# Query and key projections of a hybrid decoder: high and low part of the input in one 512-column matmul

## The chip, the cores and the metric

The kernel runs on one core of a Trainium2 chip. The metric is device time in microseconds (us) of one execution; the time before is the median of 3 runs. One execution was also recorded by the hardware profiler, and everything said of the inside of the kernel is read from that record.

## The reference, cut to what matters

Two layers work on a sequence of 256 tokens with width 1024. Each layer normalises its input, multiplies it by one wide matrix, feeds the column groups of the product to three kinds of heads, and maps the heads' output back into the residual. All arrays are float32.

```python
D_MODEL = 1024; BATCH = 1; SEQ = 256; DEPTH = 2; HEAD_DIM = 64
A_HEADS = 8; B_HEADS = 4; C_HEADS = 4
SPLIT_SIZES = [A_WIDTH] * 4 + [B_WIDTH] * 4 + [C_WIDTH] * 5 + [C_HEADS, C_HEADS]
...
def hybrid_layer(x, norm_w, w_in, conv_w, conv_b, gate_bias, ret_norm_w, mlstm_norm_w, w_out):
    h = rmsnorm(x, norm_w)
    proj = jnp.matmul(h, w_in).astype(jnp.float32)
    (aq, ak, av, ag, bq, bk, bv, bg, cq, ck, cv, co, cg, ci, cf) = jnp.split(proj, cuts, axis=-1)
    ya = moba_attention(split_heads(aq, A_HEADS), split_heads(ak, A_HEADS), split_heads(av, A_HEADS))
    ya = merge_heads(ya) * jax.nn.silu(ag)
    yb = retention(rotate(split_heads(bq, B_HEADS), pos), rotate(split_heads(bk, B_HEADS), pos),
                   split_heads(bv, B_HEADS))
    yb = head_norm(yb, ret_norm_w) * jax.nn.silu(bg)
    qk = jax.nn.silu(causal_dwconv(jnp.concatenate([cq, ck], axis=-1), conv_w, conv_b))
    ...
    yc = mlstm(split_heads(cq_c, C_HEADS), split_heads(ck_c, C_HEADS), split_heads(cv, C_HEADS), i_pre, f_pre)
    yc = head_norm(yc * split_heads(jax.nn.sigmoid(co), C_HEADS), mlstm_norm_w) * jax.nn.silu(cg)
    y = jnp.concatenate([ya, yb, yc], axis=-1)[:, :s].astype(x.dtype)
    return x + jnp.matmul(y, w_out)
```

With 256 tokens the block-sparse attention (A) is causal softmax attention over one block with a distance bias, retention (B) is one chunk, and the mLSTM (C) is computed by the kernel over the whole sequence at once.

## The kernel before, in words

**Split matmuls.** The large products are made with a faster float32 format of the TensorE (`float32r`). To keep the precision, each operand is split into a high part, rounded to that format by an ACT copy, and a low part, the remainder, by a DVE subtraction: `hi` and `lo` for the weights, `xh` and `xl` for the input (`split_x`, L416), `yh` and `yl` for the heads' output. A product is then three matmuls into the same PSUM bank: high by high, high by low, low by high.

**Weights.** `CHUNKS` (L38) cuts the columns of the input matrix into 17 pieces a layer, and the output matrix into 4, in the order in which they are worked through. `loader` (L378) fetches each piece by DMA into one of three `raw` tiles; `splitter` (L434) makes `hi` (ACT) and `lo` (DVE) of it in two halves of 1024 columns, in three tiles each, so it can be at most three chunks ahead of the TensorE.

**Projection.** `project` (L560) walks over the chunks of a layer. The query and key chunks (aq0, ak0, bq, bk, cq, ck, aq1, ak1; 256 columns each) are made transposed, channels in partitions and the 256 tokens along the free axis: the weights are the stationary operand, the input is the moving one. For each of 8 k-tiles and each of the two halves of 128 channels there are three matmuls of 256 columns (L586 to L590), and both halves go into one PSUM bank of 512 columns. The first pair of layer 0 (i = 0, 1) is worked through together as its inputs arrive. The other chunks (cvif, bvco, av, cgbg, ag) are wide: the input is stationary, the weights move, 512 columns at a time (264 for cvif), and a chunk takes two banks. The output projection of layer 0 again moves 256 columns.

**PSUM.** There are eight banks: four with the tag `pj` for projections and four with the tag `mx` for everything else (scores, transposes, head outputs).

**Evacuation.** When a query or key chunk is done, `evac_aqk` (L714), `evac_bqk` (L973) or `evac_cqk` (L842) takes it out of its bank, once the row norm of the layer is known (event `rs`; for B also `cs`), since the norm's factor is multiplied in here. A: a DVE product into a `t512` tile. B: four ACT copies of 32 partitions, which swap the halves of each head for the rotation, and a DVE product into a second `t512` tile. C: a DVE product into the convolution's buffer `cpad`. Then `stack_w` and `stack_m` (L738, L750) split the result again into `st`, `zu` and `zd` tiles for the score matmuls of `dots` (L772). The copies in there are made with `CP` (L267), which lets ACT or DVE do it.

**Order.** The order on each engine is not written down line by line. Every piece of work is a generator, and a list scheduler (`Sched`, L111) with a cost for each instruction picks the one that could start first, with a priority as tie-breaker, while the program is built; the engines then run their instructions in this fixed order. It counts a matmul as max(107, columns / 2.4) + 3 ns (L274). Tiles and banks are handed out by `acq` in the order of asking and given back with `sc.release`. An evacuation starts with priority -1, ahead of the splits (0, or 6 where they are far ahead), and goes to 2 when it has freed its bank.

All instructions pass through helpers, so the profile puts TensorE matmuls on L280, transposes on L285, VectorE on L259, ScalarE on L265 and DMAs on L288. Tiles tell them apart.

Of the kernel before, what the change touches and what calls it, by code (L numbers as in the profile page):

```python
# [11 lines left out]
F32R = mybir.dt.float32r  # L12
AF = mybir.ActivationFunctionType
OP = mybir.AluOpType
AX = mybir.AxisListType

S = 256
D_ = 1024
EPS = 1e-6
KT = 8  # L20
# [208 lines left out]
def trunk(ctx: ExitStack, tc: tile.TileContext, xp: bass.AP, w: bass.AP, fn: bass.AP,  # L229
# [5 lines left out]
    sc = Sched()  # L235

    def sb_tile(shape, name, dt=F32):
        return cp.tile(shape, dt, name=name)
# [11 lines left out]
    def V(name, out, *a, after=None, fast=False, **k):  # L250
        n = _n(a[0]) if name == "tensor_reduce" else _n(out)
        cost = n / (1.92 if fast else 0.96) + 69
        if name in ("tensor_scalar", "scalar_tensor_tensor"):
            cost += 61 * (isap(a[1]) + (isap(a[2]) if name == "tensor_scalar" else 0))
        if name == "tensor_tensor_reduce":
            cost = n / 1.3
        if name == "reciprocal":
            cost = 6.4 * n + 69
        return op("dve", cost, lambda: getattr(nc.vector, name)(out, *a, **k), after)  # L259
# [30 lines left out]
    def wait(ev):  # L290
        return ("wait", ev)
# [4 lines left out]
    def acq(tag):  # L296
        return ("acq", tag)
# [4 lines left out]
    x = px[:, P_N:].rearrange("p (k t) -> p k t", t=S)  # L302
# [5 lines left out]
    vc = sb_tile([128, 2, 4, 65], "vc")  # L308
    vb = sb_tile([128, 2, 4, HD], "vb")
    cpad = sb_tile([128, 4, 3 + S], "cpad")  # L310
    xh = sb_tile([128, KT, S], "xh", F32R)
    xl = sb_tile([128, KT, S], "xl", F32R)
    yh = sb_tile([128, KT, S], "yh", F32R)
    yl = sb_tile([128, KT, S], "yl", F32R)
    sel = sb_tile([128, 4, 128], "sel", F32R)
# [7 lines left out]
    cr = sb_tile([128, S], "cr")  # L323
# [45 lines left out]
    def E(*key):  # L369
        if key not in evs:  # L370
            evs[key] = Event()
        return evs[key]

    raws, his, los = {}, {}, {}
    at_chunk = [0]
# [184 lines left out]
    def project():  # L560
        for l in range(DEPTH):
# [3 lines left out]
            while c < len(CHUNKS):  # L565
                name, cols, k0, k1 = CHUNKS[c]
                i = base + c
                n = len(cols)
                if name[1] in "qk":
                    m = 2 if i == 0 else 1  # L570
                    ii = range(i, i + m)
                    at_chunk[0] = i + m - 1
                    ps = []
                    for q in ii:
                        p = yield acq("pj")
                        ps.append(p)
                    if i:
                        for q in ii:
                            yield wait(E("w", q, 0))
                    hv = [his[q][:, :2048].rearrange("p (k c) -> p k c", k=KT) for q in ii]  # L580
                    lv = [los[q][:, :2048].rearrange("p (k c) -> p k c", k=KT) for q in ii]
                    for k in range(KT):
                        yield wait(E("x", l, k))
                        for z in range(m):
                            yield wait(E("wk", z, k) if i == 0 else E("w", i + z, k // 4))
                            for t in range(2):  # L586
                                cs = slice(t * 128, (t + 1) * 128)
                                for q, (a, b) in enumerate(((hv[z], xh), (hv[z], xl), (lv[z], xh))):
                                    e = yield M(ps[z][:, t * 256:(t + 1) * 256], a[:, k, cs], b[:, k, :],
                                                k + t + q == 0, k == KT - 1 and q == 2)  # L590
                    for z, q in enumerate(ii):
                        sc.release("hi", his.pop(q), e)
                        sc.release("lo", los.pop(q), e)
                        nm = names[c + z]
                        sc.spawn(EVAC[nm[:2]](l, nm, ps[z]), -1, e)
                    c += m
                else:
                    ps = []
                    for b in range(2):
                        p = yield acq("pj")  # L600
                        ps.append(p)
                    parts = 2 if name.endswith("_0") else 1
                    for j in range(parts):
                        i = base + c + j
                        at_chunk[0] = i
                        _, _, k0, k1 = CHUNKS[c + j]
                        yield wait(E("w", i, 0))
                        h, lo = his[i], los[i]
                        hv = h[:, :(k1 - k0) * n].rearrange("p (k c) -> p k c", c=n)
                        lv = lo[:, :(k1 - k0) * n].rearrange("p (k c) -> p k c", c=n)  # L610
                        for k in range(k0, k1):
                            yield wait(E("w", i, (k - k0) * 2 // (k1 - k0)))
                            for b in range(2):
                                bs = slice(b * 128, (b + 1) * 128)
                                for q, (a, r) in enumerate(((xh, hv), (xh, lv), (xl, hv))):
                                    e = yield M(ps[b][:, :n], a[:, k, bs], r[:, k - k0, :], k == 0 and q == 0,
                                                k == KT - 1 and q == 2)
                        sc.release("hi", h, e)
                        sc.release("lo", lo, e)
                        del his[i], los[i]  # L620
                    sc.spawn(EVAC[name[:2]](l, name, ps), -1, e)
                    c += parts
# [88 lines left out]
    def row(a):  # L711
        return rrow.unsqueeze(1).to_broadcast([128, 2, S])

    def evac_aqk(l, name, p):  # L714
        yield wait(E("rs", l))
        t = yield acq("t512")
        if name[1] == "q":
            yield wait(E("tab"))
            for u in range(2):
                j = T_QS + 2 * int(name[2]) + u  # L720
                e = yield V("scalar_tensor_tensor", b2(t)[:, u], b2(p)[:, u], tb[:, j:j + 1], rrow, op0=OP.mult,
                            op1=OP.mult)
        else:
            e = yield V("tensor_tensor", b2(t), b2(p), row(0), op=OP.mult)
        sc.release("pj", p, e)
        yield prio(2)
        yield from (stack_w if name[1] == "q" else stack_m)(l, name, t)
        if name[1] == "k":
            g = int(name[2])
            yield wait(E("qk", l, f"aq{g}"))  # L730
            box = [0]
            for u in range(2):
                sc.spawn(pair_a(l, g, u, box), 2)
# [105 lines left out]
        sc.release("mx", pt, e)  # L839
        sc.set(done, e)  # L840

    def evac_cqk(l, name, p):  # L842
        t = 0 if name == "cq" else 2
        yield wait(E("rs", l))
        if l:
            yield wait(E("conv", l - 1, name))
        e = yield V("tensor_tensor", cpad[:, t:t + 2, 3:], b2(p), row(0), op=OP.mult)
        sc.release("pj", p, e)
        yield prio(2)
        z = yield acq("t512")  # L850
        zv = b2(z)
        for u in range(2):
            o = P_CW + l * 16 + (t + u) * 4
            ob = P_CB + l * 4 + t + u
            yield A(zv[:, u], cpad[:, t + u, 3:], AF.Identity, scale=pr[:, o + 3:o + 4], bias=pr[:, ob:ob + 1])
            for j in (2, 1, 0):
                e = yield V("scalar_tensor_tensor", zv[:, u], cpad[:, t + u, j:j + S], pr[:, o + j:o + j + 1], zv[:, u],
                            op0=OP.mult, op1=OP.add)
        sc.set(E("conv", l, name), e)
        th = yield acq("t512")  # L860
        yield A(th, z, AF.Tanh, scale=0.5)
        e = yield V("scalar_tensor_tensor", th, th, 1.0, z, op0=OP.add, op1=OP.mult)
        sc.release("t512", z, e)
        yield from (stack_w if name == "ck" else stack_m)(l, name, th)
# [105 lines left out]
        sc.release("sb", wt, e)  # L970
        sc.set(done, e)

    def evac_bqk(l, name, p):  # L973
        yield wait(E("cs", l))
        yield wait(E("tab2"))
        sw = yield acq("t512")
        for c in range(4):
            d = c ^ 1
            e0 = yield A(sw[d * 32:(d + 1) * 32, :], p[c * 32:(c + 1) * 32, :], AF.Copy)
        r_ = yield acq("t512")  # L980
        e = yield V("tensor_tensor", b2(r_), b2(p), cr.unsqueeze(1).to_broadcast([128, 2, S]), op=OP.mult)
        sc.release("pj", p, e)
        yield prio(2)
        yield V("tensor_tensor", b2(sw), b2(sw), sr.unsqueeze(1).to_broadcast([128, 2, S]), op=OP.mult)
        e = yield V("tensor_tensor", r_, r_, sw, op=OP.add)
        sc.release("t512", sw, e)
        yield from (stack_w if name == "bk" else stack_m)(l, name, r_)
        if name == "bk":
            yield wait(E("qk", l, "bq"))
            sc.spawn(group_b(l), 2)  # L990
# [180 lines left out]
```

## Time and profile before

| what | value |
|---|---|
| median of 3 runs | 305.57 us (305.52 to 305.85) |
| the profiled execution | 305.33 us |
| its span, first to last instruction | 303.6 us |
| instructions | 5195 |
| query and key matmuls of 256 columns (`pj<-xh,hi`, `pj<-xh,lo`, `pj<-xl,hi`) | 3 x 256 |
| wide matmuls of 512 columns on the input | 3 x 128 |

In the views, PE is the TensorE's matmuls, PEld its weight loads, DVE the VectorE, ACT the ScalarE, POOL the GpSimd, SP the queue that issues the DMAs. A row of the timeline gives start and duration in us, engine, line, operation and output<-inputs with the shapes; a row of the groups gives the total in us and the mean in ns of one, and then the idle time of the engine ahead of it. `x3` is a count. A row of the waits has the waiting engine, tile and line, what it waited for, and total, times and longest in us.

The query and key chunks lie at 4 to 44 us and 75 to 98 us in layer 0, and at 152 to 191 and 224 to 243 in layer 1; the wide chunks lie between and behind them, the output projections at 127 to 151 and from 272.

### The profile page before, as it was taken

Reading aid. Unit: us, or ns where it says so; the run is one execution under the profiler, and the core shown is the slowest. Engines: PE = TensorE matmul, PEld = TensorE weight load, DVE = VectorE, ACT = ScalarE, POOL = GpSimd, SP = SyncE. Lnnn points to the kernel's source line nnn. Section 1 sums busy time; section 2 is a strip of 40 time slices with the busy share of each in tenths; the row PEclk is TensorE's granted clock in tenths of the full one; section 3 lists DMA queues with packets and bytes.
Section 4 is the critical chain, followed back from the end, with each engine's and each line's share of the span. In section 5 each row is a group of like instructions: output and inputs, shape, how many; then the busy total and the mean of one; then the engine's idle time right before and its main releaser. Section 6 shows DMA issues by size and latency. Waiting matters only on the chain.

```text
span 303.6 us, 5195 instructions
## 1 busy us (share of the span) xinstructions
PE 294.3 (97%) x2016; PEld 270.5 (89%) x2016; DVE 251.3 (83%) x523; ACT 187.6 (62%) x311; POOL 15.0 (5%) x19
## 2 busy tenths in 40 slices
PE   8899999999999999999999999999999999999992
PEld 6899999887999888899999999988899988888881
DVE  3969799998989998766889799998988998767553
ACT  5958975997244656535656879487445475664332
POOL 5000000000002020000020000000002002000010
PEclk9999999999999999999999999999999999999997
DMA  6999256545620444841617706547340536250003
GB/s 201 380 384 369 123 173 245 178 139 211 221 85 0 140 138 138 270 147 21 260 15 263 244 39 188 217 151 252 137 167 2 157 123 201 83 202 1 0 2 138
DMA packets 9098, 48.62 MB, mean 160 GB/s; under 512 B 1009, under 2 KB 1905, under 8 KB 4081
## 3 DMA queue, kind: packets, MB, share of 16 engines
q1 hardware_dynamic: 9072, 48.28, 45.9%
q8 instruction: 16, 0.26, 0.3%
q14 instruction: 10, 0.07, 0.1%
HBM read 47.23 MB, written 1.05 MB: 159 GB/s over the span
## 4 chain that ended last, share of the span: by engine, by line
PE 72%; DVE 12%; ACT 8%; issue 4%; DMA 1%; POOL 1%; SPq 1%; POOLq 0%; DVEq 0%; ACTq 0%
PE pj L280 58%; PE mx L280 10%; PE mx L285 4%; DVE lo L259 3%; ACT hi L265 3%; DVE sb L259 2%; DVE small L259 2%; DVE st L259 1%; DMA px<-xp 1%; ACT sb L265 1%; ACT t L265 1%; DVE t L259 1%; ACT L265 1%; SPq L288 1%; DVE et L259 1%
## 5 line engine op out<-in xcount | busy, mean ns | idle before, releaser
L259 DVE TENSOR_TENSOR lo<-raw,hi 128x1024 fp32r<-128x1024 f32 (+2 forms) x96 | 102.5, 1086 | 9.8 <-ACT hi L265 9.5
L265 ACT ACTIVATE hi<-raw 128x1024 fp32r<-128x1024 f32 (+2 forms) x96 | 87.8, 945 | 23.8 <-PE pj L280 11.4
L280 PE MATMUL pj<-xh,hi 128*128 128x256 f32 x256 | 73.7, 288 | 0.5 <-ACT hi L265 0.5
L280 PE MATMUL pj<-xh,lo 128*128 128x256 f32 x256 | 73.8, 288 | 0.3 <-DVE lo L259 0.3
L280 PE MATMUL pj<-xl,hi 128*128 128x256 f32 x256 | 73.1, 286 | 0.0
L280 PE MATMUL pj<-hi,xh 128*128 128x512 f32 (+1 forms) x160 | 59.8, 374 | 0.0
L280 PE MATMUL pj<-lo,xh 128*128 128x512 f32 (+1 forms) x160 | 59.6, 373 | 0.0
L280 PE MATMUL pj<-hi,xl 128*128 128x512 f32 (+1 forms) x160 | 59.3, 371 | 0.0
L280 PEld LDWEIGHTS pj<-xh,hi 128*128 128x128 f32 x256 | 49.6, 194 | 1.6 <-ACT hi L265 1.5
L280 PEld LDWEIGHTS pj<-xh,lo 128*128 128x128 f32 x256 | 49.5, 193 | 0.8 <-DVE lo L259 0.7
L280 PEld LDWEIGHTS pj<-xl,hi 128*128 128x128 f32 x256 | 49.5, 193 | 0.1
L280 PEld LDWEIGHTS pj<-hi,xl 128*128 128x128 f32 x160 | 30.1, 188 | 4.6
L280 PEld LDWEIGHTS pj<-hi,xh 128*128 128x128 f32 x160 | 30.1, 188 | 4.5
L280 PEld LDWEIGHTS pj<-lo,xh 128*128 128x128 f32 x160 | 30.1, 188 | 4.3
L265 ACT ACTIVATE sb<-sb,small 128x128 f32<-128x128 f32 (+1 forms) x48 | 18.7, 447 | 10.0 <-DVE small L259 6.4
L265 ACT ACTIVATE st<-t 64x512 fp32r<-64x512 f32 x26 | 16.1, 628 | 8.5 <-DVE t L259 8.1
L280 PE MATMUL pj<-yh,lo 128*128 128x256 f32 x56 | 16.0, 286 | 0.0
L280 PE MATMUL pj<-yh,hi 128*128 128x256 f32 x56 | 15.9, 284 | 0.0
L280 PE MATMUL pj<-yl,hi 128*128 128x256 f32 x56 | 15.8, 283 | 0.0
L280 PE MATMUL mx<-st,st 128*128 128x128 f32 (+1 forms) x64 | 15.4, 274 | 0.0
L1061 POOL TENSOR_TENSOR small<-small,mhalf 128x8 f32<-128x8 f32 x4 | 6.6, 1639 | 178.3 <-DVE small L259 178.3
L280 PEld LDWEIGHTS mx<-st,st 128*128 128x128 f32 x64 | 12.2, 190 | 0.3
(146 smaller groups left out, 479.7 us busy)
## 6 DMA issues: line engine op xcount, KB each, us to landing
raw<-w SPq DMA_DIRECT2D x37, 1024.0 KB, 4.9
raw<-w SPq DMA_DIRECT2D x2, 1056.0 KB, 5.5
raw<-w SPq DMA_DIRECT2D x6, 256.0 KB, 5.4
raw<-w SPq DMA_DIRECT2D x2, 512.0 KB, 7.0
tb<-tab SPq DMA_DIRECT2D x1, 960.0 KB, 9.9
px<-xp SPq DMA_DIRECT2D x3, 256.0 KB, 4.7
tb<-tab SPq DMA_DIRECT2D x1, 514.0 KB, 7.9
raw<-w SPq DMA_DIRECT2D x4, 128.0 KB, 2.7
```

Source lines behind the costliest of these rows:

```text
L259: return op("dve", cost, lambda: getattr(nc.vector, name)(out, *a, **k), after)
L265: return op("act", cost, lambda: nc.scalar.activation(out, in_, func, **k), after)
L280: return op("pe", cost, lambda: nc.tensor.matmul(out, a, b, start=start, stop=stop, skip_group_check=True), after)
L285: return op("pe", 110.0, lambda: nc.tensor.transpose(out, in_, idn))
L288: return op("sp", cost, lambda: nc.sync.dma_start(out, in_))
L1061: yield G(1600, lambda: nc.gpsimd.tensor_tensor(vs, vs, mhalf[:, :8], op=OP.pow))
```

## The change

The high and low part of the input lie side by side in one tile `xx`, `[high | low]` for each k-tile, 512 columns. For every query and key chunk but the first pair (i > 1), each k-tile and channel half has two matmuls: the weights' high part on all 512 columns, and the weights' low part on the 256 columns of `xh`, which adds to the second half of the same bank. So each half of 128 channels has a bank of its own, whose left half holds high by high and whose right half holds the two small products. A new generator `summed` adds the two: for each bank an ACT copy of the right half into a `t512` tile, and a DVE add of the left half to it. The evacuations then read that tile in SBUF, not the bank; A and B work in it in place. The fourth chunk of layer 0 (i = 3, bk) takes its two banks from `mx`, the others from `pj`.

```diff
-    xh = sb_tile([128, KT, S], "xh", F32R)
-    xl = sb_tile([128, KT, S], "xl", F32R)
+    xx = sb_tile([128, KT, 2 * S], "xx", F32R)
+    xh, xl = xx[:, :, :S], xx[:, :, S:]
...
-                if name[1] in "qk":
+                if name[1] in "qk" and i > 1:
+                    at_chunk[0] = i
+                    tag = "mx" if i == 3 else "pj"
+                    ps = []
+                    for t in range(2):
+                        p = yield acq(tag)
+                        ps.append(p)
+                    yield wait(E("w", i, 0))
+                    hv, lv = [t[i][:, :2048].rearrange("p (k c) -> p k c", k=KT) for t in (his, los)]
+                    for k in range(KT):
+                        yield wait(E("x", l, k))
+                        yield wait(E("w", i, k // 4))
+                        for t in range(2):
+                            cs = slice(t * 128, (t + 1) * 128)
+                            yield M(ps[t], hv[:, k, cs], xx[:, k, :], k == 0, False)
+                            e = yield M(ps[t][:, S:], lv[:, k, cs], xh[:, k, :], False, k == KT - 1)
+                    sc.release("hi", his.pop(i), e)
+                    sc.release("lo", los.pop(i), e)
+                    sc.spawn(summed(l, name, ps, tag), -1, e)
+                    c += 1
+                elif name[1] in "qk":
...
+    def summed(l, name, ps, tag):
+        t = yield acq("t512")
+        for u in range(2):
+            h = b2(ps[u])
+            yield A(b2(t)[:, u], h[:, 1], AF.Copy)
+            e = yield V("tensor_tensor", b2(t)[:, u], h[:, 0], b2(t)[:, u], op=OP.add)
+            sc.release(tag, ps[u], e)
+        yield from EVAC[name[:2]](l, name, t, "t512")
...
-    def evac_aqk(l, name, p):
+    def evac_aqk(l, name, p, tag="pj"):
         yield wait(E("rs", l))
-        t = yield acq("t512")
+        t = p if tag == "t512" else (yield acq("t512"))
...
-    def evac_cqk(l, name, p):
+    def evac_cqk(l, name, p, tag="pj"):
...
-        sc.release("pj", p, e)
+        sc.release(tag, p, e)
...
-    def evac_bqk(l, name, p):
+    def evac_bqk(l, name, p, tag="pj"):
...
-        r_ = yield acq("t512")
-        e = yield V("tensor_tensor", b2(r_), b2(p), cr.unsqueeze(1).to_broadcast([128, 2, S]), op=OP.mult)
-        sc.release("pj", p, e)
+        r_ = p if tag == "t512" else (yield acq("t512"))
+        e = yield V("tensor_tensor", b2(r_), b2(p), cr.unsqueeze(1).to_broadcast([128, 2, S]), op=OP.mult,
+                    after=e0 + Sched.LAT if p is r_ else None)
+        if p is not r_:
+            sc.release("pj", p, e)
```

More of the change, by code (lines that the diff above doesn't have):

```diff
@@ L724, in evac_aqk @@
             e = yield V("tensor_tensor", b2(t), b2(p), row(0), op=OP.mult)
-        sc.release("pj", p, e)
+        if p is not t:
+            sc.release("pj", p, e)
         yield prio(2)
@@ L979, in evac_bqk @@
             e0 = yield A(sw[d * 32:(d + 1) * 32, :], p[c * 32:(c + 1) * 32, :], AF.Copy)
-        r_ = yield acq("t512")
-        e = yield V("tensor_tensor", b2(r_), b2(p), cr.unsqueeze(1).to_broadcast([128, 2, S]), op=OP.mult)
-        sc.release("pj", p, e)
+        r_ = p if tag == "t512" else (yield acq("t512"))
+        e = yield V("tensor_tensor", b2(r_), b2(p), cr.unsqueeze(1).to_broadcast([128, 2, S]), op=OP.mult,
+                    after=e0 + Sched.LAT if p is r_ else None)
+        if p is not r_:
+            sc.release("pj", p, e)
         yield prio(2)
```

## The prediction

> **What bounds the kernel now.** I read the first and fourth part of the page first.
>
> ```profile
> PE 294.3 (97%) x2016; PEld 270.5 (89%) x2016; DVE 251.3 (83%) x523; ACT 187.6 (62%) x311; POOL 15.0 (5%) x19
> PE 72%; DVE 12%; ACT 8%; issue 4%; DMA 1%; POOL 1%; SPq 1%; POOLq 0%; DVEq 0%; ACTq 0%
> ```
>
> TensorE (PE) is busy for 97% of the span and carries 72% of the chain that ended last. Busy time overstates it, since a matmul's record overlaps the next one, so I asked the list of waits what TensorE and its weight loads (PEld) ever waited for.
>
> ```profile
> PEld pj L280 <- ACT hi L265: 1.5, 2, 0.8
> PEld pj L280 <- DVE lo L259: 1.5, 4, 0.6
> PEld mx L285 <- ACT sb L265: 0.9, 2, 0.5
> PEld mx L285 <- DVE small L259: 0.7, 1, 0.7
> ```
>
> The four largest causes after the warm-up, in total us, times and longest: under 5 us in all, in a span of 303.6. Matmuls follow one another almost without a hole, so a matmul made shorter can shorten the kernel. The view by stretches shows who would stop that (columns: length, then busy us of PE, PEld, DVE, ACT, with counts).
>
> ```profile
> 15.00:40.00 25.00, 25.00 (x211) 25.00 (x211) 20.58 (x35) 17.78 (x27) 0.71 (x1) 1.00 0.70 269
> 40.00:75.00 35.00, 34.58 (x204) 30.23 (x203) 33.26 (x69) 29.46 (x48) 0.00 (x0) 1.00 0.59 195
> 75.00:110.00 35.00, 35.00 (x261) 33.08 (x259) 33.42 (x84) 16.25 (x28) 1.65 (x1) 1.00 0.40 137
> 151.00:186.00 35.00, 34.59 (x289) 34.12 (x288) 30.98 (x64) 25.87 (x40) 1.61 (x1) 1.00 0.45 152
> 186.00:224.00 38.00, 38.00 (x235) 33.86 (x234) 36.26 (x64) 22.71 (x32) 0.00 (x0) 1.00 0.51 173
> ```
>
> VectorE (DVE) is nearly as full as TensorE: 33.26 of 35 us in 40 to 75, 36.26 of 38 in 186 to 224. So two engines are close to the bound, and the change takes work from one and gives work to the other.
>
> **What a matmul costs.** The start-to-start distance is the price, not the duration in the record. In the timeline of TensorE, the end of the last 256-column query or key chunk and the wide chunk behind it, and then the end of another wide chunk:
>
> ```profile
> 242.65 0.28 PE L280 MATMUL pj<-xh,lo 128*128 128x256 f32 x1
> ...
> 243.37 0.28 PE L280 MATMUL pj<-xh,lo 128*128 128x256 f32 x1
> 243.49 0.40 PE L280 MATMUL pj<-hi,xh 128*128 128x512 f32 x1
> 243.72 0.40 PE L280 MATMUL pj<-lo,xh 128*128 128x512 f32 x1
> ...
> 124.63 0.39 PE L280 MATMUL pj<-hi,xl 128*128 128x512 f32 x1
> ...
> 127.35 0.39 PE L280 MATMUL pj<-hi,xl 128*128 128x512 f32 x1
> 127.58 0.28 PE L280 MATMUL pj<-yh,hi 128*128 128x256 f32 x1
> 127.69 0.28 PE L280 MATMUL pj<-yl,hi 128*128 128x256 f32 x1
> ```
>
> From 242.65 to 243.49 lie seven 256-column matmuls in 0.84 us: 120 ns each. From 124.63 to 127.35 lie twelve 512-column ones in 2.72 us: 227 ns each. Two 256s cost 240 and one 512 costs 227, so 13 ns go with each pair joined. Where sizes alternate, the first 512 behind a 256 lasts 0.23 us (243.49 to 243.72), and the first 256 behind a 512 lasts 0.11 (127.58 to 127.69). On the rounding of these rows I take 227 to 235 for the 512 and 113 to 120 for the 256.
>
> The Trainium skill, "TensorE: Matmul & The Clock Gate", section Back-to-back issue gap, gives N/2.4 + 2.5 ns for an isolated warm matmul; by it three 256s are 328 ns, a 512 and a 256 are 325, and the whole change would be worth an estimated 0.6 us. The trace differs: 120 ns where that gives 109, 227 where it gives 216.
>
> **The change part by part.** *Matmuls.* Chunks with i > 1 take the new path: six in layer 0 (bq, bk, cq, ck, aq1, ak1), eight in layer 1. Each has 8 k-tiles by 2 column halves, 16 sites, so 14 x 16 = 224 sites. A site had three 256s (360 ns) and gets a 512 and a 256. By the transition rows that is at worst 235 + 120 = 355, at best 227 + 113 = 340; I take the middle, 348, since steady 227 and 120 make 347. So 12 ns a site: 224 x 12 = **2.7 us less on TensorE**, with bounds 224 x 5 = 1.1 and 224 x 20 = 4.5. One weight load less a site counts nothing extra: the loads run beside the matmuls, and the start-to-start distances contain them.
>
> *Adding the halves.* Per chunk `summed` adds two ACT copies and two DVE adds of 128x256 out of PSUM. The nearest rows of the same kind are the split of y:
>
> ```profile
> L265 ACT ACTIVATE yh<-mx 128x256 fp32r<-128x256 f32 x8 | 2.9, 382 | 7.1 <-PE mx L285 5.8 <-DVE yl L259 1.3
> L259 DVE TENSOR_TENSOR yl<-mx,yh 128x256 fp32r<-128x256 f32 x8 | 3.2, 420 | 4.7 <-ACT yh L265 4.6
> L259 DVE TENSOR_TENSOR lo<-raw,hi 128x1024 fp32r<-128x1024 f32 x76 | 91.4, 1217 | 8.5 <-ACT hi L265 8.2
> L265 ACT ACTIVATE t<-pj 32x512 f32<-32x512 f32 x16 | 9.1, 586 | 1.6 <-PE pj L280 1.4
> L265 ACT ACTIVATE st<-t 64x512 fp32r<-64x512 f32 x26 | 16.1, 628 | 8.5 <-DVE t L259 8.1
> ```
>
> 28 x 0.382 = 10.7 us more on ACT, 28 x 0.420 = 11.8 us more on DVE, nothing removed in exchange: the first instruction of each evacuation stays and now reads SBUF. For the rotary copies of bq and bk that is 586 (from PSUM) against 628 ns (from SBUF), at most 16 x 0.04 = 0.7 us more on ACT. DVE's total becomes about 263 us, still below 303.6, ACT's 199. Neither lies on the path as long as the lo halves, which DVE makes and every chunk waits for, are ready ahead. How far ahead they are decides what the 11.8 us cost. Three places, each a DVE split row and the first matmul that uses it:
>
> ```profile
> 30.91 3.84 ACT L265 ACTIVATE t<-pj 32x512 f32<-32x512 f32 x7 [0.51 <-PE pj L280]
> 34.77 2.99 ACT L265 ACTIVATE hi<-raw 128x1024 fp32r<-128x1024 f32 x3
> 36.86 2.35 DVE L259 TENSOR_TENSOR lo<-raw,hi 128x1024 fp32r<-128x1024 f32 x2
> 38.33 0.28 PE L280 MATMUL pj<-xh,hi 128*128 128x256 f32 x1
> 63.65 2.36 DVE L259 TENSOR_TENSOR lo<-raw,hi 128x1024 fp32r<-128x1024 f32 x2
> 68.16 0.39 PE L280 MATMUL pj<-hi,xh 128*128 128x512 f32 x1
> 78.18 1.19 DVE L259 TENSOR_TENSOR lo<-raw,hi 128x1024 fp32r<-128x1024 f32 x1
> 98.59 0.40 PE L280 MATMUL pj<-hi,xh 128*128 128x512 f32 x1
> ```
>
> At ck of layer 0 the first half is split at 36.86 + 1.22 = 38.08 and used at 38.33: 0.25 us of cover. At the second half of av it is 64.87 against 68.16: 3.3 us. At cgbg it is 79.37 against 98.59: 19 us. So cover is thin up to about 75 us and ample later in the layer.
>
> *ck of layer 0* is where I charge something. TensorE comes there earlier by three chunks (bq, bk, cq: 48 sites x 12 ns = 0.58 us), 0.33 us more than the cover; and the hi split of ck (34.77) is queued on ACT behind the rotary copies, to which bq and bk add four copies of 0.38, less the 0.51 of idle time ahead of them: another 1.0 at most. A stall of 0.33 to 1.3 us, or none if the written-out order puts the split first: I take **0.8**.
>
> *The rest of the cover.* Up to 75 the four early chunks add 8 x 0.42 = 3.4 us of DVE work, for which 15 to 40 has 25 - 20.58 = 4.4 idle and 40 to 75 has 1.7. I charge nothing there, covered by those 4.4 us; if they can't be filled, a lag up to 3.3 us is still covered at av. In layer 1 the six chunks of 151 to 190 add 5.0 us, against 4.0 idle up to 186 and 1.7 up to 224, so DVE runs nearly full but not over.
>
> *Banks.* A chunk takes two pj banks of four (bk of layer 0 two mx banks), not one, and gives them back after ACT 0.38 + DVE 0.42 for each half, 1.6 us, behind at most a pair of lo splits (2.36): 4.0 us. A chunk of 16 sites lasts 5.6. So the next chunk but one finds its banks, and I charge nothing. `summed` also frees them before the row norm is known, earlier than now at the head of layer 1.
>
> *Sum.* The profiled execution took 305.33 us, its span 303.6, with 1.7 around it; the median of the runs is 305.57, 0.24 more. 305.33 - 2.7 + 0.8 = 303.4, on the scale of the median **303.7 us**.
>
> **Rivals.** *All of the gain, or the better pace.* If the order covers ck, 2.7 lands whole: 302.9; with the best pace, 340 ns a site, 301.1. For it: the later cover of 19 us. Chance 0.12.
>
> *No gain to be seen.* If the 13 ns belong to a stream of equal matmuls, not to the instruction saved, alternation gives them back: 355 ns a site, 1.1 us, and the 0.8 at ck leaves 305.3. For it: the 512 behind a 256 is the slower one. The skill's formula, above, ends in the same place. Chance 0.13.
>
> *Slower: VectorE becomes the bound in 40 to 75.* DVE has 1.7 us free in these 35 us and ACT 5.5, and the chunks bk to ck hand them their adds just ahead. It decides when DVE's lag passes the 3.3 us of av. If none of the 3.4 us finds an idle place and the bank reads wait on each other (ACT copy, then DVE add, 0.8 us of latency for each of the four chunks, 3.2 us), the lag is 6.6 and the stall 3.3. Together with 0.8 at ck, against the whole 2.7: 305.57 + 1.4 = 307.0. For it: DVE's 95% share. Against it: ACT can take over some of the copies for which the scheduler picks either engine, and the order is worked out anew with the adds in it. The Trainium skill, "Trainium Kernel Development and Optimization", section Best Practices, warns of exactly this: faster matmuls do not speed up the evacuation of PSUM. This trace agrees as far as DVE's shares go. Chance 0.17.
>
> *Slower: banks.* It decides when the return of two banks takes longer than the 5.6 us of a chunk. With two pairs of splits ahead of the adds it is 4.7 + 1.6 = 6.3, so TensorE waits 0.7 us; at half of the 14 chunks that is 4.9 against 2.7, 307.8. Against it: DVE would have to be that far behind again and again. Chance 0.08.
>
> **How the numbers follow.** The forecast itself has 0.5: 303.7, from 302.9 (nothing at ck) to 304.8 (355 ns a site and the 0.33 us at ck). A difference of 0.2%, 0.6 us, is about what a measurement of this kernel can tell from none. Faster by more: forecast 0.50 plus whole gain 0.12 = 0.62. Same: 0.13. Slower: 0.17 + 0.08 = 0.25. The range runs from 301.3, just short of the best pace, to 307.0, the DVE rival's value; it leaves out the banks (0.08), the worse part of the DVE rival and the very best pace, together under 0.2.
>
> **What would show it.** In the profile after: 512-column matmuls pj<-xx or xh with hi, 224 of them, starting 227 to 235 ns before the 256 behind them, which holds 113 to 120; 224 fewer matmuls and weight loads (1792); DVE near 263, ACT near 198. A hole on TensorE at ck of layer 0 with ACT hi or DVE lo as its releaser. The first layer's end should move by 0.5 or less, the second layer should be some 1.5 us shorter. Wrong: a site at 355 or more; new waits of TensorE on DVE lo around 50 to 75; waits whose releaser is the add of the halves, which would be the banks.

## The result and the profile after

The changed kernel takes 303.91 us (median of 22 runs), the kernel before 305.64 in the same comparison: a ratio of 0.9938, with a 95% interval of 0.9923 to 0.9954, by which it takes 1.9 us less (1.4 to 2.4). The profiled execution took 304.55 us, its span 302.8.

The page of the changed kernel, first and fourth part:

```profile
PE 293.0 (97%) x1792; PEld 258.7 (85%) x1792; DVE 259.4 (86%) x551; ACT 195.2 (64%) x339; POOL 16.7 (6%) x19
PE 82%; ACT 9%; issue 2%; DMA 2%; POOL 1%; DVE 1%; SPq 1%; POOLq 0%
```

There are 224 matmuls and weight loads fewer. DVE has 28 instructions more and ACT 28 more. TensorE's share of the chain that ended last rose from 72 to 82%, DVE's fell from 12 to 1%. DVE does more, and yet stands less in the way; the order of the whole program was made anew, and the runs below show what that is worth. The groups of the page show the added instructions (two more of each kind work on the `mx` banks):

```profile
L265 ACT ACTIVATE t<-pj 128x256 f32<-128x256 f32 x26 | 9.8, 378 | 18.4 <-PE pj L280 18.4
L259 DVE TENSOR_TENSOR t<-pj,t 128x256 f32<-128x256 f32 x26 | 10.9, 418 | 1.8 <-ACT t L265 1.5
```

378 and 418 ns each, against the 382 and 420 of the sum. Now the price of a site, in the timeline of TensorE at the head of layer 1:

```profile
156.48 0.40 PE L280 MATMUL pj<-xx,hi 128*128 128x512 f32 x1
156.71 0.28 PE L280 MATMUL pj<-xx,lo 128*128 128x256 f32 x1
156.83 0.39 PE L280 MATMUL pj<-xx,hi 128*128 128x512 f32 x1
157.06 0.27 PE L280 MATMUL pj<-xx,lo 128*128 128x256 f32 x1
157.17 0.40 PE L280 MATMUL pj<-xx,hi 128*128 128x512 f32 x1
157.40 0.28 PE L280 MATMUL pj<-xx,lo 128*128 128x256 f32 x1
157.52 0.39 PE L280 MATMUL pj<-xx,hi 128*128 128x512 f32 x1
```

Three sites in 1.04 us, 347 ns each. Over all sites the median distance to the next start is 233 ns from the 512 and 117 from the 256, so 350, where three 256s took 360. And ck of layer 0, where the sum charged 0.8 us:

```profile
35.06 1.22 DVE L259 TENSOR_TENSOR lo<-raw,hi 128x1024 fp32r<-128x1024 f32 x1
38.91 0.39 PE L280 MATMUL pj<-xx,hi 128*128 128x512 f32 x1
```

Its first low half is done at 36.28 and used at 38.91: 2.6 us of cover instead of 0.25, and no stall. The new order puts ck's hi split between the rotary copies, not behind them.

**A measure by stages.** The start of a run is not the same each time: the first matmul of bq starts between 18.1 and 21.3 us in the profiled executions of this study, since at about 8 us the TensorE waits for the first inputs, with 0.7 to 2.3 us from one matmul to the next. In five of the thirteen executions the granted clock then stands at 0.50 for 3.4 us, from 11 or 12 us on; these five have bq at 20.0 to 21.3, the others at 18.1 to 19.5. So I compare from there on, with four starts of matmuls read from each timeline: the first of bq, the first and the last of layer 0's output projection, and the first of layer 1's. The last column is the time of whole runs. Each row is one execution, and a difference of 0.4 us between two rows can be a single wait that comes and goes, as a case below shows.

| kernel | bq to output projection | projection of layer 0 | layer 1 | median, us |
|---|---|---|---|---|
| before | 109.02 | 24.03 | 120.46 | 305.64 |
| changed | 108.25 | 24.03 | 119.92 | 303.91 |
| adds alone | 108.83 | 28.61 | 121.05 | 310.50 |
| no DVE add | 107.72 | 24.02 | 119.87 | 303.87 |
| DVE twice, scheduler told | 114.42 | 26.43 | 121.72 | 314.32 |
| sizes in pairs | 108.23 | 24.03 | 120.44 | 304.21 |
| 256s, same order | 108.65 | 24.03 | 120.55 | 305.35 |
| DVE twice, same order | 113.97 | 24.03 | 125.37 | 314.20 |
| no add, same order | 107.68 | 24.03 | 119.61 | 303.92 |
| bk in pj | 110.07 | 24.04 | 120.05 | 305.85 |
| 64 columns more, same order | 110.23 | 24.03 | 122.36 | 308.41 |
| before with DVE more | 113.24 | 24.03 | 123.71 | 313.24 |
| measured costs | 108.13 | 24.03 | 122.38 | 306.95 |

The change takes 0.77 us from layer 0 and 0.54 from layer 1. Layer 1, with 128 of the 224 sites, was forecast to give 1.5.

### The profile page after: what moved, and what is told of

Same layout as the page of the kernel before. It is cut to its first block, busy times and chain, and to the rows that moved or that the text cites. A ratio compares the mean times of both kernels' runs of the same rounds, so it can differ in the third digit from the quotient of the medians.

```text
span 302.8 us, 4794 instructions
## 1 busy us (share of the span) xinstructions
PE 293.0 (97%) x1792; PEld 258.7 (85%) x1792; DVE 259.4 (86%) x551; ACT 195.2 (64%) x339; POOL 16.7 (6%) x19
## 4 chain that ended last, share of the span: by engine, by line
PE 82%; ACT 9%; issue 2%; DMA 2%; POOL 1%; DVE 1%; SPq 1%; POOLq 0%
PE pj L280 64%; PE mx L280 14%; ACT t L265 4%; PE mx L285 4%; ACT hi L265 3%; DMA px<-xp 2%; POOL small L488 1%; DVE lo L259 1%; ACT sb L265 1%; SPq L288 1%; ACT st L265 1%; POOL small L547 0%; ACT xx L265 0%; ACT raw L265 0%; POOLq L1201 0%
## 5 line engine op out<-in xcount | busy, mean ns | idle before, releaser
L280 PE MATMUL pj<-hi,xx 128*128 128x512 f32 (+1 forms) x320 | 93.1, 372 | 0.0
L280 PE MATMUL pj<-xx,hi 128*128 128x512 f32 (+1 forms) x272 | 88.0, 377 | 0.8 <-ACT hi L265 0.8
L280 PE MATMUL pj<-xx,lo 128*128 128x256 f32 x240 | 69.2, 288 | 0.3 <-DVE lo L259 0.2
L280 PEld LDWEIGHTS pj<-hi,xx 128*128 128x128 f32 x320 | 57.5, 188 | 9.1
L280 PE MATMUL pj<-lo,xx 128*128 128x512 f32 (+1 forms) x160 | 59.7, 373 | 0.0
L280 PEld LDWEIGHTS pj<-xx,hi 128*128 128x128 f32 x272 | 50.1, 193 | 10.1 <-ACT hi L265 1.9
L280 PEld LDWEIGHTS pj<-xx,lo 128*128 128x128 f32 x240 | 45.9, 191 | 0.8 <-DVE lo L259 0.7
L280 PEld LDWEIGHTS pj<-lo,xx 128*128 128x128 f32 x160 | 30.1, 188 | 4.5
L265 ACT ACTIVATE t<-t 32x512 f32<-32x512 f32 (+1 forms) x20 | 12.5, 629 | 0.3
L259 DVE TENSOR_TENSOR t<-pj,t 128x256 f32<-128x256 f32 x26 | 10.9, 418 | 1.8 <-ACT t L265 1.5
```

What stands on the lines that cost most here:

```text
L265: return op("act", cost, lambda: nc.scalar.activation(out, in_, func, **k), after)
L280: return op("pe", cost, lambda: nc.tensor.matmul(out, a, b, start=start, stop=stop, skip_group_check=True), after)
```

## The experiments

My theory after the result: the matmuls bring the gain, and the adds cost nothing, since DVE has cover. The rival: the adds cost 0.8 us or more, which the matmuls more than pay. A second rival: DVE is the bound.

**The adds without the saving.** Each site keeps three 256s:

```diff
-                            yield M(ps[t], hv[:, k, cs], xx[:, k, :], k == 0, False)
+                            yield M(ps[t][:, :S], hv[:, k, cs], xh[:, k, :], k == 0, False)
+                            yield M(ps[t][:, S:], hv[:, k, cs], xl[:, k, :], False, False)
```

> The new banks, the side-by-side tile, the ACT copies and the DVE adds stay, but each site keeps three 256-column matmuls, so the saving of the TensorE is taken out and the price of the rest stands alone. My theory: the added work is hidden (in the changed kernel the splits are done 1.5 to 18 us ahead of their first use, and DVE rises only to 259 us), so the time is that of the kernel before, 305.6 within 0.6. Rival, the one of the prediction's sum: the adds cost about 0.8 us and the saving was larger than the result, so 306.4. Rival, DVE is the bound: 307 or more.

Measured: 310.50, ratio 1.0142 (1.0101 to 1.0183), against every theory but the second rival. But the stages do not say that DVE is the bound everywhere: up to the output projection this kernel is as fast as the one before (108.83 against 109.02), and all the loss of layer 0, 4.6 us, lies in the first 9 us behind that point. TensorE there:

```profile
126.09 0.39 PE L280 MATMUL pj<-hi,xx 128*128 128x512 f32 x1
126.32 1.03 PE L285 MATMUL mx<-tb,t 128*128 128x128 f32 x8
127.88 0.38 PE L280 MATMUL pj<-yh,hi 128*128 128x256 f32 x1 [0.53 <-ACT yh L265]
...
129.77 0.38 PE L280 MATMUL pj<-yh,hi 128*128 128x256 f32 x1 [0.52 <-ACT yh L265]
131.66 0.38 PE L280 MATMUL pj<-yl,hi 128*128 128x256 f32 x1 [1.50 <-DVE yl L259]
```

and DVE in the same stretch:

```profile
127.86 0.48 DVE L259 SCALAR_TENSOR_TENSOR yl<-mx,px,yh 128x256 fp32r<-128x256 f32 x1 [0.59 <-ACT yh L265]
128.26 1.22 DVE L259 TENSOR_TENSOR lo<-raw,hi 128x1024 fp32r<-128x1024 f32 x1
129.40 0.68 DVE L259 SCALAR_TENSOR_TENSOR t<-t,pj 128x512 f32<-128x512 f32 x1
129.99 1.22 DVE L259 TENSOR_TENSOR lo<-raw,hi 128x1024 fp32r<-128x1024 f32 x1
131.13 0.87 DVE L259 SCALAR_TENSOR_TENSOR yl<-mx,px,yh 128x256 fp32r<-128x256 f32 x2
```

The order written for this kernel transposes y (`mx<-tb,t`) right before the output projection, and puts two weight splits, 1.22 us each, between the low parts of y that it waits for. Behind the wait of 1.50 the granted clock falls to 0.50, from 132.2 to 135.7, so that work of about 1.7 us takes 3.4: some 1.7 us of the loss are the clock and not the wait itself. In the changed kernel four of these transposes stand at 119.80, 7.5 us ahead of the projection at 127.29. So this run mixes two things: the price of the adds and another order. Runs further below, named "same order", hold the order of the changed kernel on every engine; the next three do not.

**No DVE add** (the low products left out):

```diff
-            yield A(b2(t)[:, u], h[:, 1], AF.Copy)
-            e = yield V("tensor_tensor", b2(t)[:, u], h[:, 0], b2(t)[:, u], op=OP.add)
+            e = yield A(b2(t)[:, u], h[:, 0], AF.Copy)
```

> Leaves out the sum of the halves: ACT copies the left half of each bank, and the two small products in the right half are dropped; the 28 DVE adds (11 us) are gone, all matmuls stay. My theory: DVE's adds lie beside the matmuls, so the time is that of the changed kernel, 303.9 within 0.6. Rival: the adds hold 0.8 us, so 303.1. Rival, DVE is the bound: 11 us less of its work brings more than 2 us, under 302.

Measured: 303.87, ratio 0.9938 (0.9911 to 0.9966), the changed kernel's own. By stages 0.53 and 0.05 us less, in an order that the scheduler made anew. The whole runs can't tell the adds from nothing, give or take 1 us.

**DVE twice, scheduler told**: one more DVE instruction of 128x256 ahead of each add.

```diff
             yield A(b2(t)[:, u], h[:, 1], AF.Copy)
+            yield V("tensor_tensor", b2(t)[:, u], b2(t)[:, u], b2(t)[:, u], op=OP.max)
```

> A second DVE instruction of 128x256 (the maximum of the copied half with itself) goes ahead of each add, 28 more, about 11 us of DVE work, and the return of each bank comes 0.4 us later. My theory: still hidden mostly, DVE would reach 270 of 303 us; 303.9 to 304.9, with waits of the TensorE on DVE lo first in layer 0 ahead of 75 us. Rival, DVE is near the bound already: 2 us or more, 306 or over.

Measured: 314.32, ratio 1.0273 (1.0231 to 1.0315), 10.4 us over the changed kernel: the rival. The first 28 DVE instructions cost nothing that shows, the next 28 cost 0.37 us each on the average. But that average covers several things: the transposes of y at the end of layer 0 wait 0.92 and 2.87 us for DVE, the granted clock is 0.50 from 131.3 to 138.1, and three times (0.94, 0.67 and 1.12 us) a projection waits for a DVE instruction on `t`, that is for a bank given back late.

**Sizes in pairs**: both 512s of a k-tile, then both 256s.

```diff
-                            yield M(ps[t], hv[:, k, cs], xx[:, k, :], k == 0, False)
-                            e = yield M(ps[t][:, S:], lv[:, k, cs], xh[:, k, :], False, k == KT - 1)
+                            yield M(ps[t], hv[:, k, cs[t]], xx[:, k, :], k == 0, False)
+                        for t in range(2):
+                            e = yield M(ps[t][:, S:], lv[:, k, cs[t]], xh[:, k, :], False, k == KT - 1)
```

> Only the order within a k-tile changes: both 512-column matmuls first, then both 256-column ones. In the changed kernel's trace a 512 behind a 256 starts the next matmul after 233 ns, a 512 behind a 512 after 227; a 256 behind a 512 takes 113 to 117, a 256 behind a 256 120. Theory that the change of size costs: two sites take 233 + 227 + 114 + 120 = 694 ns where they now take 2 x 350 = 700, about 6 ns by 112, 0.7 us faster, 303.2. Rival, each matmul has its price whatever stands before it: 303.9.

Measured: 304.21, ratio 0.9948 (0.9919 to 0.9978). The theory missed. In this trace two sites take 697 ns by medians (a 512 behind a 256 and one behind a 512, then a 256 behind a 512 and one behind a 256: 233, 231, 115.5 and 118), against 700, and the 0.3 us that this could give is not to be seen. The scheduler also moved some instructions of DVE and ACT in this run.

**256s in the changed kernel's order.** Two 256s are issued within one step of the scheduler, at the cost of the 512, so that all engines keep their order:

```diff
-                            yield M(ps[t], hv[:, k, cs], xx[:, k, :], k == 0, False)
+                            yield M2(ps[t], hv[:, k, cs], xx[:, k, :], k == 0)
...
+        def both():
+            nc.tensor.matmul(out[:, :S], a, b[:, :S], start=start, stop=False, skip_group_check=True)
+            return nc.tensor.matmul(out[:, S:], a, b[:, S:], start=False, stop=False, skip_group_check=True)
```

> The changed kernel with one thing taken back: in the place of each 512-column matmul stand two 256-column ones, with the scheduler told the same cost, so every engine keeps the order of the changed kernel. My theory: the saving of the matmuls by itself is what the trace shows, 360 ns a site against 350, 224 x 10 ns = 2.2 us, and the 5 us that the run with the adds alone lost were its order (its waits at the end of layer 0), so 303.9 + 2.2 = 306.1. Rival, the prediction's 12 ns: 306.6. Rival, the adds need the saving, order or not: 309 or more.

Measured: 305.35, ratio 0.9980 (0.9949 to 1.0011). The same matmuls, copies and adds as in the first run, in another order: 5.2 us less. So what the 310.50 lost were its order, with the 1.7 us of lower clock in it. And the saving by itself is 305.35 - 303.91 = 1.4 us (the ratios differ by 0.42%, 1.3 us, give or take 1.1 by the two intervals), by stages 0.40 + 0.63 = 1.0; less than the 2.2 that 10 ns a site make. Where the rest goes is read at the end of the next section. With the adds but without the saving the kernel stands at the time of the kernel before, so banks, adds and new order together cost nothing that can be measured.

**DVE twice in the changed kernel's order**, the second instruction hidden from the scheduler:

```diff
+            def twice(o=b2(t)[:, u], i=h[:, 0]):
+                nc.vector.tensor_tensor(o, o, o, op=OP.max)
+                return nc.vector.tensor_tensor(o, i, o, op=OP.add)
```

> The changed kernel in its own order, with a second DVE instruction of 128x256 issued directly ahead of each of the 28 adds and not told to the scheduler: 28 x 0.35 = 9.8 us more on DVE. My theory: the cover is thin at one place, the end of layer 0, where in the changed kernel the last low part of y is ready 1.15 us ahead of the first matmul of the output projection; 12 of the 28 (4.2 us) lie ahead of it, so 2 to 4 us are lost there, and up to 1 elsewhere: 306 to 308.5. Rival, the 314.3 of the run with the scheduler told was DVE's load, not its order: 312 or more. Rival, all of it is covered: 304.5 or less.

Measured: 314.20, ratio 1.0254 (1.0216 to 1.0291). So the added load costs this much without a new order too, though the total equals that of the run with the scheduler told only by chance, since the stages differ (layer 1 lost 1.8 us there and loses 5.5 here). My theory of the place was wrong. Layer 0's loss is there before its output projection begins, and layer 1 loses as much. The lo halves stay ahead nearly everywhere (av of layer 0 by 4.5 us). What is late are the score matmuls of the heads. DVE in this run, then TensorE:

```profile
29.34 0.42 DVE L743 TENSOR_TENSOR t<-t 128x256 f32<-128x256 f32 x1
29.87 0.42 DVE L744 TENSOR_TENSOR t<-pj,t 128x256 f32<-128x256 f32 x1
...
35.46 0.68 DVE L259 TENSOR_TENSOR zu<-t,st 64x512 fp32r<-64x512 f32 x1
```

```profile
34.74 0.22 PE L280 MATMUL mx<-st,st 128*128 128x128 f32 x1
36.19 0.33 PE L280 MATMUL mx<-zu,st 128*128 128x128 f32 x1 [1.23 <-DVE zu L259]
```

and the same two steps in the changed kernel:

```profile
33.26 0.68 DVE L259 TENSOR_TENSOR zu<-t,st 64x512 fp32r<-64x512 f32 x1
35.97 0.28 PE L280 MATMUL mx<-zu,st 128*128 128x128 f32 x1
```

There `zu` is done 2.0 us ahead of its matmul; here it is 2.2 us later and the TensorE waits 1.23 for it, in the middle of cq, with everything queued behind. What follows costs more than the wait. This run, and then the changed kernel, over the same 3 us (length; busy us of PE, PEld, DVE, ACT and POOL with counts; granted clock; DMA):

```profile
38.00:41.00 3.00, 3.00 (x12) 2.71 (x12) 3.00 (x6) 2.93 (x5) 0.00 (x0) 0.50 0.03 8
```

```profile
38.00:41.00 3.00, 3.00 (x20) 2.60 (x19) 3.00 (x13) 2.92 (x5) 0.00 (x0) 1.00 0.75 243
```

At a granted clock of 0.50, which lasts from 37.7 to 41.1, the TensorE gets 12 matmuls done in place of 20. Of the 11.2 us that this execution loses by stages, about 1.7 are the clock. Waits of the TensorE's weight loads in this run:

```profile
PEld mx L285 <- ACT sb L265: 5.8, 9, 1.3
PEld mx L280 <- DVE zu L259: 1.7, 2, 1.5
PEld pj L280 <- ACT hi L265: 1.6, 3, 0.8
```

The first row is the transposes of the softmax, whose ACT input comes out of a DVE reduction, the second the wait shown above; the third is at the start of the run and was there before. The added instruction holds DVE for 0.52 us, not 0.35, since the add behind it needs its result (29.34 to 29.87): 28 x 0.52 = 14.6 us for a loss of 10.3.

**No add, same order** (low products left out): a one-column DVE copy in the place of each add, in the same scheduler step.

```diff
-            yield A(b2(t)[:, u], h[:, 1], AF.Copy)
-            e = yield V("tensor_tensor", b2(t)[:, u], h[:, 0], b2(t)[:, u], op=OP.add)
+            yield A(b2(t)[:, u], h[:, 0], AF.Copy)
+            def one(o=b2(t)[:, u, 0:1], i=h[:, 0, 0:1]):
+                return nc.vector.tensor_copy(o, i)
+            e = yield op("dve", S / 0.96 + 69, one)
```

> Leaves out the sum of the halves (ACT copies the left half, the small products are dropped); the changed kernel in its own order, with one-column DVE copies in the place of the 28 adds. My theory: 28 x 0.35 us less on DVE bring nothing that a measurement can tell, 303.9 within 0.6. Rival, the adds hold 0.8 us or more on the path: 303.1 or less.

Measured: 303.92, ratio 0.9941 (0.9916 to 0.9966): no difference, give or take 0.9 us by the two intervals, so the rival's 0.8 is not quite excluded by the whole runs. By stages it is 0.57 and 0.31 us less. Laid beside the changed kernel matmul by matmul, 0.39 of that is one wait for the row norm at 23.6 us, which the runs with more DVE work in the same order lack as well; it belongs to the execution and not to the adds. That leaves about 0.5 us for them at most.

**bk in pj:**

```diff
-                    tag = "mx" if i == 3 else "pj"
+                    tag = "pj"
```

> One part undone: bk of layer 0 takes its two banks from the four of the projections, like the other chunks. At 25 us two of those four still hold aq0 and ak0, whose evacuation waits for the row norm, and the other two hold bq. Theory that banks can bind: the TensorE waits about 2 us for them in layer 0, 305.5 to 306.5. Rival, the waiting is filled by other work in the order that the scheduler then finds: 303.9 within 0.6.

Measured: 305.85, ratio 0.9983 (0.9958 to 1.0008): the first theory in time. TensorE, from bq's last matmul to bk's first, and later:

```profile
26.63 0.28 PE L280 MATMUL pj<-xx,lo 128*128 128x256 f32 x1
27.03 0.47 PE L280 MATMUL pj<-xx,hi 128*128 128x512 f32 x1
...
38.99 0.84 PE L285 MATMUL mx<-tb,sb 128*128 128x128 f32 x3 [0.62 <-ACT sb L265]
```

The hole at bk itself is 0.40 where 0.12 is normal. The rest of the 1.8 us of layer 0 comes later, 0.62 of it in the wait at 38.99. The scheduler made another order, so how much of it is banks and how much order stays open. Without the two `mx` banks, and in the order that goes with that, the change gives no gain that can be measured.

**64 columns more on DVE**, in the changed kernel's order:

```diff
+                nc.vector.tensor_tensor(o[:, :64], o[:, :64], o[:, :64], op=OP.max)
                 return nc.vector.tensor_tensor(o, i, o, op=OP.add)
```

> The changed kernel in its own order with a small DVE instruction of 128x64 ahead of each of the 28 adds, not told to the scheduler: about 0.13 us each, 3.6 us in all. Without the adds the kernel took 303.92, with them 303.91, with twice their DVE work 314.2. Theory of an edge: the changed kernel stands just where DVE's cover ends, and from there each us on DVE costs about one: 303.9 + 3.6 = 307.5. Rival, a cover of a few us is left and the loss begins beyond it: 304.5 or less.

Measured: 308.41, ratio 1.0084 (1.0062 to 1.0106). The small instruction takes 0.32 us from start to start, not 0.13, again for the dependence behind it:

```profile
31.31 0.23 DVE L743 TENSOR_TENSOR t<-t 128x64 f32<-128x64 f32 x1
31.64 0.42 DVE L744 TENSOR_TENSOR t<-mx,t 128x256 f32<-128x256 f32 x1
```

So 28 x 0.32 = 9.0 us of DVE time cost 4.5 us, and 14.6 cost 10.3. Between the two each us costs (10.3 - 4.5) / (14.6 - 9.0) = 1.04; with the intervals of the two runs it can be 0.7 to 1.2. If the loss falls along that line, it reaches zero at 2.5 to 5 us of DVE time: a cover of that size over both layers is an estimate from two doses, and no run lies between it and zero. Neither expectation was right: an edge at zero would have given 303.9 + 9.0 = 312.9, and 304.5 is passed by far.

Matched with the changed kernel matmul by matmul, this run loses 4.4 us from bq on, with no fall of the clock: 3.2 us ahead of the small matmuls and transposes of the heads (2.1 at the transposes of the softmax alone), 0.7 at a projection that waits for a bank held by one of the adds (44.97), and nothing at a weight split.

**The kernel before with DVE more**, in its own order: the maximum of each half with itself behind the first product of the evacuation, hidden from the scheduler.

```diff
+                r = fn()
+                for o in halves:
+                    r = nc.vector.tensor_tensor(o, o, o, op=OP.max)
```

> The kernel before in its own order, with 28 DVE instructions of 128x256 (the maximum of each half of the evacuated tile with itself) issued directly behind the evacuation's first product in the 14 chunks, not told to the scheduler: the same 9.8 us of DVE work as the adds, no other part of the change. Theory that the change used up a cover which the kernel before had: most of it is hidden, 306 to 308. Rival, DVE's chain was at its edge before already and only an order made with the adds in it hides them: 313 or more.

Measured: 313.24 against 306.06 for the kernel before in this comparison, ratio 1.0236 (1.0216 to 1.0256). A chunk's two instructions and the wait ahead of them hold DVE for about 0.8 us, 11.2 in all, for 7.2 lost: here too a cover of a few us, 4 if each us beyond it costs one. The two longest waits are for reductions (1.5 and 1.6 us, `small`), and the next is at ck of layer 0, where the sum of the prediction had read 0.25 us of cover:

```profile
40.70 0.38 PE L280 MATMUL pj<-xh,lo 128*128 128x256 f32 x1 [1.01 <-DVE lo L259]
```

The kernel before would probably have lost several us to the adds in its own order. What hides them is the order of the changed kernel (305.35 for the 256s in it), and not any order made with the adds in it: the first run had one as well, and lost 5 us.

**Measured costs in the scheduler:**

```diff
-            cost = max(107.0, n / 2.4) + 3
+            cost = max(99.0, n / 2.4) + 13
...
-            cost = 2 * max(107.0, n * 2 / 2.4 / 1.0) + 3
+            cost = max(107.0, n * 4 / 2.4) + 3
```

> The changed kernel, with the scheduler's cost of a matmul set to what the trace shows: 120 ns for 256 columns and 226 for 512 in place of 110 and 216, 111 for the small head matmuls in place of 217. Theory that the order leaves time on the table, since the scheduler counts on a faster projection than there is: fewer waits of the TensorE, 303.4 or less. Rival, an order is as good as another within a us or two of luck: between 303 and 306.

Measured: 306.95, ratio 1.0030 (1.0011 to 1.0050), 3 us over the changed kernel, just beyond the rival's 306. Layer 0 is as fast (108.13), layer 1 is 2.5 us longer, with weight loads that wait for softmax and gate inputs:

```profile
PEld mx L285 <- ACT sb L265: 2.5, 5, 1.1
PEld mx L285 <- DVE small L259: 1.4, 1, 1.4
```

It may be that the too short costs served as a margin, since by them the TensorE comes later to each head matmul than the scheduler counts on; no run separates that from luck. No version of this study that computes everything beats the changed kernel.

## Why the prediction was right

The time came out at 303.91 where 303.7 was forecast, in the direction and nearly in the size. Step by step:

- *TensorE is the bound, and the distance between starts is the price.* Right. The matmuls alone, with the order held, are worth 1.4 us (0.3 to 2.5) by whole runs and 1.0 by stages.
- *12 ns a site, 2.7 us.* Too much. By medians the sites take 350 ns, within the bounds but 2 ns over the value taken, so 2.2 us, and 1.0 to 1.4 of that arrive. By the formula of the Trainium skill ("TensorE: Matmul & The Clock Gate", section Back-to-back issue gap) a site would save an estimated 2.5 ns; these traces show more, by medians 360 against 350.
- *0.8 us for a stall at ck.* Wrong: no stall, since the new order covers it by 2.6 us. The reading of ck was right for the order before, where 11 us more of DVE make the TensorE wait 1.0 us there; it failed because a place was carried over into an order that was still to be made. This error and the one before nearly cancel: 2.7 - 0.8 was forecast, 1.0 to 1.4 from the matmuls and a remainder of order within the noise were found. That the sum came out so close is in part luck.
- *The adds are charged at nothing, 10.7 us on ACT and 11.8 on DVE, hidden by the splits' lead.* The charge was right, the reason only in part. Taking the DVE adds away brings nothing that shows; but the cover that decides is not the lead of the weight splits, 1.5 to 20 us. In the changed kernel it is that of the head matmuls, which the TensorE meets in a fixed order between the projections, 2.0 us at `zu` in layer 0. By the estimate above a few us of DVE time more, 2.5 to 5, use it up.
- *The rival that VectorE becomes the bound*, with a share of 0.17: it did not happen, but its price was far too small. 14.6 us more of DVE cost 10.3. Its place, av in 40 to 75, was wrong as well.
- *Banks charged at nothing.* Right for the change as it is, with bk in `mx`. With bk in `pj` the whole gain was gone, by banks and order together, and with more DVE work single waits for a bank appear.
- *That the scheduler makes the order anew with the adds in it* stood in the text as a help against the DVE rival. It was the main thing, and it can go either way: the same instructions in two orders, both made with the adds in them, took 305.35 and 310.50.

The 2.2 us of shorter sites shrink to 1.0 by stages for two reasons, which show when the changed kernel is laid beside the run with 256s in its order, matmul by matmul. First, a site saves less than the medians say. The 512 takes 237 ns to the next start on the average, where its two 256s take 242, since some 512s last 230 ns and others 240; the 256 behind it takes 121 against 124. That is 7 ns a site, 1.5 us in all. Second, 0.5 us goes back in three waits ahead of transposes of the softmax. The longest is in layer 0, first in the changed kernel, then the same transposes with 256s:

```profile
43.77 0.27 PE L285 MATMUL mx<-tb,sb 128*128 128x128 f32 x1
44.34 0.44 PE L285 MATMUL mx<-tb,sb 128*128 128x128 f32 x2 [0.30 <-ACT sb L265]
```

```profile
46.39 0.70 PE L291 MATMUL mx<-tb,sb 128*128 128x128 f32 x3
```

The faster TensorE waits there for the ACT copy `sb`; the slower one finds it ready. The other two lie at 181 and 186 us, 0.1 each. The largest waits of the changed kernel's weight loads, the warm-up left out, show it too; the second row is these transposes, and it was 1.0 with 256s in the same order:

```profile
PEld pj L280 <- ACT hi L265: 1.9, 2, 1.0
PEld mx L285 <- ACT sb L265: 1.7, 3, 0.8
PEld pj L280 <- DVE lo L259: 1.5, 4, 0.6
PEld mx L285 <- POOL small L488: 1.0, 2, 0.5
```

What stays open is what the adds hold, between nothing and 0.5 us by stages, and how much of the remaining gain over the kernel before is order and how much noise.

## What to carry to other kernels

Where two engines are both nearly full, work moved from one to the other is free only up to the second one's cover, which is how far ahead of their use its results are ready. It is read at the consumer with the least lead, here the small matmuls in between, not at the largest producer. Test it with a dose: add work that changes nothing in known amounts, with the order held, until the time bends; a removal that brings nothing says little about what an addition will cost. And where a program orders itself from a cost model, compare variants in the same order before giving a difference to the edit: the order alone made 5 us here, more than the change. A place with little cover belongs to one order, too: it need not be there in the next.

## What was not expected of the hardware

A DVE instruction that reads what the one ahead of it on DVE just wrote starts later: 0.52 us behind a 128x256 one (median of 28), where independent ones of that size start about 0.34 apart, and 0.32 behind one of only 64 columns. Short dependent steps cost DVE far more than their columns. A 512-column matmul next to 256-column ones costs 231 to 233 ns by medians where a stream of them has 227, while the 256 behind it gets cheaper, 115.5 to 117 in place of 120, so a change of size costs almost nothing.

And a wait of the TensorE can cost more than its length. Around a wait of 1.23, 1.50 and 2.87 us (DVE twice in the same order, the adds alone, DVE twice with the scheduler told) the granted clock fell to 0.50, for 3.4, 3.4 and 6.8 us, during which matmuls took nearly twice as long. Waits of 1.5 and 1.6 us in the kernel before with more DVE work (at 77.0 and 218.2 us) were followed by no fall, so the length of one wait does not decide it, and no run here shows what does.
